# Layer B of a two-layer trunk: three direct pairs instead of four, and their low halves by accumulating DMAs instead of VectorE

## The chip, the cores and the metric

The kernel runs on one core of a Trainium2 chip. The metric is device time in microseconds of one execution. TensorE (PE in the profile) multiplies, VectorE (DVE) and ScalarE (ACT) work on what lies in SBUF and PSUM, GpSimd (POOL) does next to nothing here, SyncE (SP) issues the DMAs.

## The reference, cut to what matters

A sequence of 256 tokens, width 2048, passes two residual layers in float32, each with its norm, and a final norm:

```
p  = rms_norm(x, a_norm_g) @ a_w_in          # layer A: 2048 x 12288 -> u | v | z
x += (gelu(u) * mix(layer_norm(gelu(v))) * silu(z)) @ a_w_out
p  = rms_norm(x, b_norm_g) @ b_w_in          # layer B: 2048 x 20480 -> q,k,v three times | z
x += (attention(q, k, v; three dilations) * silu(z)) @ b_w_out
out = rms_norm(x, final_norm_g)
```

The change sits in the largest product, that with `b_w_in`: 256 x 2048 times 2048 x 20480.

## The kernel before

**Two halves of a number.** The kernel multiplies in the format fp32r. Each operand is split into a high half (the value cast to fp32r) and a low half (the value minus its high half), and `triple` (L229) makes one product of three matmuls: high times high, low times high, high times low. For weights the split is `split` (L126): ScalarE casts the raw tile to `wh`, and VectorE subtracts, `wl = raw - wh`.

**Slabs.** `slab` (L235) makes two 512-wide column blocks of the output, L and R, for both 128-token blocks. It walks over the 2048 rows of the weight in eight pairs of 128-row blocks. `load_pair` (L215) fetches a pair by two 512 KB DMAs on SP's queue into a `raw` tile of 128 x 2048 elements.

**Two kinds of pair.** A pair of kind "D" (direct) takes eight products, so 24 matmuls of 512 columns, and its weights need one cast and one subtraction of 2048 elements per partition. A pair of kind "S" takes seven products, so 21 matmuls, by a scheme in the manner of Strassen and Winograd. It needs sums of weight blocks first: VectorE makes `tsum` in three additions (L287 to L289), then 1536 elements of `raw` and 2048 of `tsum` are split, each by a cast and a subtraction. `KINDS_B` says which pairs are which and `ORDER_B` the order in which a slab walks over them. In layer B before, four of the eight are S, in the order D S D S S D S D. Layer B has 20 slabs (four quads of heads, five slabs each: three for q and k, two for v and z).

**Accumulators.** A slab holds seven accumulators, out of eight buffers in PSUM. When the last S pair has had its products, `early` (L261) combines three of them; the rest of the combinations (L309 to L317) follow at the slab's end, and `done` takes each result out on ScalarE.

**What sets the order.** The kernel is written in the Tile layer, whose scheduler fixes each engine's order at build time; an engine works its list in that order and waits on semaphores. Two pools bound how far work runs ahead of TensorE, and both hand out their buffers in turn, each new tile waiting for the one four allocations back:

```
wraw = ctx.enter_context(tc.tile_pool(name="wraw", bufs=NRAW))     # NRAW = 4: raw and tsum
wsp = ctx.enter_context(tc.tile_pool(name="wsp", bufs=NW))         # NW = 4: pairs wh, wl
```

A D pair takes one `raw` and one pair of `wh`, `wl`; an S pair takes two of each (`raw` and `tsum`; `wh`, `wl` and `vh`, `vl`). Small work between the slabs (transposes of q and k, scores, softmax, the product with v) is put between pairs by `later` and `tick`.

Of the kernel before, what the change touches and what calls it, by code (L numbers as in the profile page):

```python
# [9 lines left out]
F32 = mybir.dt.float32  # L10
F32R = mybir.dt.float32r
AF = mybir.ActivationFunctionType
ALU = mybir.AluOpType
AX = mybir.AxisListType

P = 128
D = 2048
S = 256
NT = S // P
EPS = 1e-6  # L20
AW = 4096
# [8 lines left out]
CW = 512  # L30
# [8 lines left out]
WARM2 = 11  # L39
NST = 11  # L40
NW = 4
NRAW = 4


KINDS_A, ORDER_A = "DDDSDSDS", (0, 1, 2, 3, 4, 5, 7, 6)
KINDS_B, ORDER_B = "DSDSDSDS", (0, 1, 2, 3, 5, 4, 7, 6)

# [21 lines left out]
def trunk(ctx, tc, x, a_norm_g, a_w_in, a_ln_g, a_ln_b, a_w_s, a_b_s, a_w_out,  # L69
          b_norm_g, b_w_in, b_w_out, final_norm_g, consts, out):  # L70
    nc = tc.nc
# [6 lines left out]
    opp = ctx.enter_context(tc.tile_pool(name="opp", bufs=8))  # L78
# [7 lines left out]
    def st(shape, name, dtype=F32):  # L86
        return stp.tile(shape, dtype, name=name, tag="st")
# [4 lines left out]
    ident = const.tile([P, P], F32, name="ident")  # L92
    tril = const.tile([P, P], F32, name="tril")
    dm0 = const.tile([P, NT, S], F32, name="dm0")
    dm12 = const.tile([P, 2, P], F32, name="dm12")
    rows = const.tile([P, P], F32, name="rows")
    cols = const.tile([P, P], F32, name="cols")
# [33 lines left out]
    class Operand:  # L131
# [9 lines left out]
        def alloc(self, kg):  # L141
            for part, d in (("h", self.hi), ("l", self.lo)):
                d[kg] = opp.tile([P, 13, P], F32R, name=f"{self.name}{part}{kg}", tag="op")
            self.at = {k: v for k, v in self.at.items() if k[0] // (KG // 2) != kg}
# [31 lines left out]
        def sums(self, kg, f, n):  # L176
            kinds = self.kinds[kg * (KG // 2) : (kg + 1) * (KG // 2)]
            sf = st([P, 6, P], f"{self.name}s")
            m = 0
            tt = nc.vector.tensor_tensor  # L180
            for i in range(KG // 2):
                q = f[:, 4 * i : 4 * i + 4, :]
                if kinds[i] == "D":
                    h = q.rearrange("p (k t) m -> p k t m", t=NT)
                    tt(out=sf[:, m : m + 2, :], in0=h[:, :, 0, :], in1=h[:, :, 1, :], op=ALU.subtract)
                    for j in range(2):
                        self.place(kg, i, ("d", j), n + m + j)
                    m += 2
                else:
                    a11, a21, a12, a22 = (q[:, b, :] for b in range(4))  # L190
                    for o, i0, i1 in ((0, a21, a22), (1, a11, sf[:, m]), (2, a21, a11), (3, a12, sf[:, m + 1])):
                        tt(out=sf[:, m + o, :], in0=i0, in1=i1, op=ALU.subtract)
                        self.place(kg, i, f"s{o + 1}", n + m + o)
                    m += 4
            split(sf[:, 0:m, :], self.hi[kg][:, n : n + m, :], self.lo[kg][:, n : n + m, :])
# [38 lines left out]

    def slab(h, w, cl, cr, dst, done, pre=None, fine=0):  # L235

# [32 lines left out]
        for n, i in enumerate(h.order):  # L269
            raw = load_pair(w, i, cl, cr, 1 if n < fine else 2)  # L270
            wh, wl = new_split()
            if h.kinds[i] != "S":
                if n >= fine:
                    split(raw, wh, wl)
# [80 lines left out]
    nc.vector.memset(ones, 1.0)  # L355
    nc.vector.memset(rows, 0.0)
    warm = small.tile([P, 1], F32, name="warm")
# [15 lines left out]
    with ExitStack() as actx:  # L373
        apool = actx.enter_context(tc.tile_pool(name="apool", bufs=1))

        xt = [st([P, NT, CW], f"x{kg}") for kg in range(4)]
# [53 lines left out]
        for c in range(0, NCH_A, 2):  # L430
# [8 lines left out]
            if c == 0:  # L439
                def pre(n):  # L440
# [13 lines left out]
                    nc.sync.dma_start(out=tril, in_=consts[:, P : 2 * P])  # L454
                    nc.sync.dma_start(out=dm0, in_=consts[:, 2 * P : 2 * P + NT * S].rearrange("p (b s) -> p b s", b=NT))
                    nc.sync.dma_start(out=dm12, in_=consts[:, 2 * P + NT * S :].rearrange("p (g s) -> p g s", g=2))
                    ssq = const.tile([P, NT, 4], F32, name="ssqa")
# [4 lines left out]
            else:  # L462
                pre = None
            slab(hA, a_w_in[0], AW + c * CW, AW + (c + 1) * CW, v2, v_done, pre, 2 if c == 0 else 0)
        mv = const.tile([P, NT, 2], F32, name="mv")
# [8 lines left out]
        for c in range(NCH_A):  # L474
# [3 lines left out]
            nc.sync.dma_start(out=wt, in_=a_w_s[0, c * G2 : (c + 1) * G2].rearrange("g t s -> t g s"))  # L478
            bs = apool.tile([P, G2, P], F32, name="bs", tag="bs", bufs=2)
            nc.sync.dma_start(out=bs, in_=a_b_s[0:1, c * G2 : (c + 1) * G2, :].broadcast_to([P, G2, P]))  # L480
# [45 lines left out]

            slab(hA, a_w_in[0], c * CW, 2 * AW + c * CW, uz, uz_done)
            g = st([P, KG, S], f"g{c}")
# [15 lines left out]


    gA = Operand("N" * (AW // P // 2), tuple(range(AW // P // 2)), "g")
    hB = Operand(KINDS_B, ORDER_B, "b")
# [110 lines left out]
    for q in range(NQUAD):  # L658
# [3 lines left out]
        for g in range(NG):  # L662
# [4 lines left out]

            slab(hB, b_w_in[0], 3 * g * D + q * CW, (3 * g + 1) * D + q * CW, qk, qk_done)
            qT, kT = st([P, KG, S], "qT"), st([P, KG, S], "kT")
# [13 lines left out]

        slab(hB, b_w_in[0], 2 * D + q * CW, 5 * D + q * CW, vs[:2], v_done)
        z = st([P, NT, CW], "zB")
# [6 lines left out]

        slab(hB, b_w_in[0], 8 * D + q * CW, 9 * D + q * CW, [vs[2], z], vz_done)

# [120 lines left out]
```

## Time and profile before

| | us |
|---|---|
| median of 3 runs (1747.61 to 1752.64) | 1751.72 |
| the profiled execution, its own time | 1750.36 |
| its span, first to last instruction | 1748.6 |
| TensorE busy in it | 1728.4 (99%) |
| VectorE busy in it | 1460.0 (83%) |
| ScalarE busy in it | 1025.9 (59%) |
| layer B's slabs, about 690 to 1625 us of the span: VectorE busy in these 935 us | 821.65 |

The profiled execution lies 1.4 us below the median, inside the spread of the runs, and 1.76 us of its time lie outside its span. The profile's busy share of TensorE counts overlapping matmuls, so it says that TensorE seldom stands still, not how fast it goes; its pace is read from the starts of successive matmuls. Names such as `bh` and `bl` are the high and low halves of layer B's input, `ah`, `gh`, `oh` those of other products.

### The profile page before, as it was taken

Reading aid. Unit: us, or ns where it says so; the run is one execution under the profiler, and the core shown is the slowest. Engines: PE = TensorE matmul, PEld = TensorE weight load, DVE = VectorE, ACT = ScalarE, POOL = GpSimd, SP = SyncE. Lnnn points to the kernel's source line nnn. Section 1 sums busy time; section 2 is a strip of 40 time slices with the busy share of each in tenths; the row PEclk is TensorE's granted clock in tenths of the full one; section 3 lists DMA queues with packets and bytes.
Section 4 is the critical chain, followed back from the end, with each engine's and each line's share of the span. In section 5 each row is a group of like instructions: output and inputs, shape, how many; then the busy total and the mean of one; then the engine's idle time right before and its main releaser. Section 6 shows DMA issues by size and latency. Waiting matters only on the chain.

```text
span 1748.6 us, 21067 instructions
## 1 busy us (share of the span) xinstructions
PE 1728.4 (99%) x8130; PEld 1434.7 (82%) x8130; DVE 1460.0 (83%) x1366; ACT 1025.9 (59%) x929; POOL 6.0 (0%) x9
## 2 busy tenths in 40 slices
PE   9999999999999999999999999999999999999998
PEld 7788888888888888788878888888888888888787
DVE  7988888999888555788989888988989988889753
ACT  7655765556566454555666555665556666556642
POOL 0000000000000000000000000000000000000000
PEclk9999999999999999999999999999999999999999
DMA  7666565555558575355656555555555456555871
GB/s 244 215 211 210 191 207 193 189 187 186 189 184 280 193 240 183 131 191 171 195 190 193 186 187 192 178 173 193 191 192 190 155 185 194 180 193 171 292 245 51
DMA packets 176404, 337.50 MB, mean 193 GB/s; under 512 B 10576, under 2 KB 14640, under 8 KB 176304
## 3 DMA queue, kind: packets, MB, share of 16 engines
q1 hardware_dynamic: 176304, 336.16, 58.1%
q8 instruction: 63, 1.03, 0.2%
q14 instruction: 37, 0.30, 0.1%
HBM read 330.35 MB, written 5.77 MB: 192 GB/s over the span
## 4 chain that ended last, share of the span: by engine, by line
PE 88%; DVE 5%; issue 2%; DMA 2%; ACT 2%; SPq 0%; ACTq 0%; DVEq 0%; POOLq 0%; POOL 0%
PE acc L231 27%; PE acc L233 27%; PE acc L232 27%; DVE wl L128 3%; DMA raw<-in_b_w_in_dram 1%; ACT wh L127 1%; PE pm L506 1%; PE sc L631 1%; PE pp L644 1%; PE po L703 1%; PE po L701 1%; PE sc L625 1%; PE tq L615 1%; DVE tsum L287 1%; PE tk L615 1%
## 5 line engine op out<-in xcount | busy, mean ns | idle before, releaser
L128 DVE TENSOR_TENSOR wl<-raw,wh 128x2048 fp32r<-128x2048 f32 (+2 forms) x306 | 633.0, 2069 | 114.9 <-ACT wh L127 112.1
L127 ACT CAST wh<-raw 128x2048 fp32r<-128x2048 f32 (+2 forms) x306 | 531.2, 1737 | 323.8 <-PE acc L232 252.5
L231 PE MATMUL acc<-wh,bh 128*128 128x512 f32 x1200 | 483.1, 403 | 3.6 <-ACT full L202 2.2
L233 PE MATMUL acc<-wl,bh 128*128 128x512 f32 x1200 | 470.2, 392 | 0.0
L232 PE MATMUL acc<-wh,bl 128*128 128x512 f32 x1200 | 468.6, 390 | 0.0
L127 ACT CAST wh<-tsum 128x2048 fp32r<-128x2048 f32 x116 | 221.7, 1911 | 209.3 <-DVE tsum L289 109.6
L128 DVE TENSOR_TENSOR wl<-tsum,wh 128x2048 fp32r<-128x2048 f32 x116 | 265.4, 2288 | 83.8 <-ACT wh L127 83.0
L231 PE MATMUL acc<-wh,ah 128*128 128x512 f32 x732 | 291.2, 399 | 2.8 <-ACT wh L127 2.8
L232 PE MATMUL acc<-wh,al 128*128 128x512 f32 x732 | 285.9, 391 | 0.7 <-DVE al L211 0.7
L233 PE MATMUL acc<-wl,ah 128*128 128x512 f32 x732 | 284.1, 391 | 2.0 <-DVE wl L128 2.0
L233 PEld LDWEIGHTS acc<-wl,bh 128*128 128x128 f32 x1200 | 225.6, 188 | 49.1 <-DVE wl L128 0.6
L231 PEld LDWEIGHTS acc<-wh,bh 128*128 128x128 f32 x1200 | 226.0, 188 | 47.3 <-ACT full L202 2.4
L232 PEld LDWEIGHTS acc<-wh,bl 128*128 128x128 f32 x1200 | 226.3, 189 | 43.7
L287 DVE TENSOR_TENSOR tsum<-raw 128x1024 f32<-128x1024 f32 x116 | 141.4, 1219 | 46.5 <-DMA raw<-in_b_w_in_dram 41.4
L231 PEld LDWEIGHTS acc<-wh,ah 128*128 128x128 f32 x732 | 138.2, 189 | 32.2 <-ACT wh L127 4.7
L233 PEld LDWEIGHTS acc<-wl,ah 128*128 128x128 f32 x732 | 137.4, 188 | 31.7 <-DVE wl L128 3.2
L232 PEld LDWEIGHTS acc<-wh,al 128*128 128x128 f32 x732 | 137.7, 188 | 28.9 <-DVE al L211 1.1
L231 PE MATMUL acc<-wh,gh 128*128 128x512 f32 x256 | 100.6, 393 | 0.0
L233 PE MATMUL acc<-wl,gh 128*128 128x512 f32 x256 | 99.8, 390 | 0.0
L232 PE MATMUL acc<-wh,gl 128*128 128x512 f32 x256 | 99.7, 389 | 0.0
L289 DVE TENSOR_TENSOR tsum<-tsum,raw 128x512 f32<-128x512 f32 x116 | 79.4, 685 | 1.0
L288 DVE TENSOR_TENSOR tsum<-tsum,raw 128x512 f32<-128x512 f32 x116 | 79.3, 683 | 0.8
(185 smaller groups left out, 1379.4 us busy)
## 6 DMA issues: line engine op xcount, KB each, us to landing
raw<-in_b_w_in_dram SPq DMA_DIRECT2D x320, 512.0 KB, 4.7
raw<-in_a_w_in_dram SPq DMA_DIRECT2D x188, 512.0 KB, 4.7
raw<-in_a_w_out_dram SPq DMA_DIRECT2D x64, 512.0 KB, 5.0
raw<-in_b_w_out_dram SPq DMA_DIRECT2D x16, 512.0 KB, 7.6
raw<-in_b_w_out_dram SPq DMA_DIRECT2D x8, 1024.0 KB, 5.1
raw<-in_a_w_in_dram SPq DMA_DIRECT2D x8, 256.0 KB, 6.1
rx<-in_x_dram SPq DMA_DIRECT2D x4, 512.0 KB, 7.6
x<-rx SPq DMA_DIRECT2D x4, 512.0 KB, 6.4
```

Of the source, the lines that this page charges most:

```text
L127: nc.scalar.copy(out=hi, in_=src)
L128: nc.vector.tensor_tensor(out=lo, in0=src, in1=hi.bitcast(F32), op=ALU.subtract)
L231: nc.tensor.matmul(acc, a[0], wh, start=start, stop=False)
L232: nc.tensor.matmul(acc, a[1], wh, start=False, stop=False)
L233: nc.tensor.matmul(acc, a[0], wl, start=False, stop=stop)
L287: tt(out=tsum[:, 0:2, :], in0=raw[:, 0:1, :].broadcast_to([P, 2, CW]), in1=raw[:, 1:3, :], op=ALU.add)
L288: tt(out=tsum[:, 2, :], in0=tsum[:, 0, :], in1=raw[:, 2, :], op=ALU.add)
L289: tt(out=tsum[:, 3, :], in0=tsum[:, 2, :], in1=raw[:, 3, :], op=ALU.add)
L506: nc.tensor.matmul(pm[:, f, t, :], v[:, t, fs], wsT[:, i, :], start=True, stop=True)
L615: nc.tensor.transpose(pt[:, f, t * P : (t + 1) * P], src[:, t, fs], ident)
L625: nc.tensor.matmul(sc[:, b, :], q[:, i, b * P : (b + 1) * P], k[:, i, :], start=True, stop=True)
L631: nc.tensor.matmul(sc[:, b, :], q[:, i, bs], k[:, i, bs], start=True, stop=True)
```

## The change

In layer B five of the eight pairs become S pairs and three stay D, in the order D S D S D S S S. For the D pairs, VectorE no longer makes the low half. ScalarE writes the high half twice, once as `wh` and once negated into `wl`, and then GpSimd issues two DMAs of 512 KB that add `raw` onto `wl` inside SBUF, one for each half of the tile. Layer A keeps its split (`DMA_A` is empty).

A group of two S pairs has 14 blocks where the largest group before had 13 (`NBLK`). To make room, `tril` and `rows` move into layer A's pool, `bs` goes from two buffers to one, and `dm0` and `dm12` are loaded after layer A into a pool of their own.

```
-KINDS_B, ORDER_B = "DSDSDSDS", (0, 1, 2, 3, 5, 4, 7, 6)
+DMA_A = ()
+DMA_B = (0, 2, 4)
+KINDS_B, ORDER_B = "SSDSDSDS", (2, 0, 4, 1, 6, 3, 5, 7)
...
             if h.kinds[i] != "S":
-                if n >= fine:
+                if n >= fine and n in dma:
+                    nc.scalar.copy(out=wh, in_=raw)
+                    nc.scalar.activation(out=wl, in_=raw, func=AF.Copy, scale=-1.0)
+                    for j in range(2):
+                        js = slice(2 * j, 2 * j + 2)
+                        nc.gpsimd.dma_start(out=wl[:, js, :], in_=raw[:, js, :], accum_op=ALU.add)
+                elif n >= fine:
                     split(raw, wh, wl)
...
-            bs = apool.tile([P, G2, P], F32, name="bs", tag="bs", bufs=2)
+            bs = apool.tile([P, G2, P], F32, name="bs", tag="bs")
...
+    bpool = ctx.enter_context(tc.tile_pool(name="bpool", bufs=1))
+    dm0 = bpool.tile([P, NT, S], F32, name="dm0")
+    dm12 = bpool.tile([P, 2, P], F32, name="dm12")
+    nc.sync.dma_start(out=dm0, in_=consts[:, 2 * P : 2 * P + NT * S].rearrange("p (b s) -> p b s", b=NT))
+    nc.sync.dma_start(out=dm12, in_=consts[:, 2 * P + NT * S :].rearrange("p (g s) -> p g s", g=2))
...
-            slab(hB, b_w_in[0], 3 * g * D + q * CW, (3 * g + 1) * D + q * CW, qk, qk_done)
+            slab(hB, b_w_in[0], 3 * g * D + q * CW, (3 * g + 1) * D + q * CW, qk, qk_done, dma=DMA_B)
```

`n` counts a pair's place in the slab, so the three D pairs stand at places 0, 2 and 4, and each has its low half made by DMA.

The first place is ScalarE where the first slab of layer B ends and the second begins. The numbers behind the names tell tiles apart; `raw_6030` before and `raw_6060` after are the weights of the new slab's first pair. Before:

```order
L127 CAST wh_5954<-tsum_5948 128x2048 [waits DVE_49,PE_49,Activation_49]
L127 CAST wh_5989<-raw_5986 128x2048 [waits DMAHW0_49,DMAHW7_49,PE_49,Activation_49]
L127 CAST wh_6033<-raw_6030 128x2048 [waits DMAHW1_49,DMAHW2_49,PE_49,Activation_49]
L127 CAST wh_6068<-raw_6065 128x1536 [waits DMAHW3_49,DMAHW4_49,PE_49,Activation_49]
L262 COPY k_5698<-acc_5749 128x512
```

After:

```order
L126 CAST wh_6011<-raw_6008 128x1536 [waits DMAHW0_49,DMAHW7_49,PE_49,Activation_49]
L126 CAST wh_6019<-tsum_6013 128x2048 [waits DVE_49,PE_49,Activation_49]
L273 CAST wh_6063<-raw_6060 128x2048 [waits DMAHW1_49,DMAHW2_49,PE_49,Activation_49]
L274 ACTIVATE wl_6064<-raw_6060 128x2048 [waits DMASW5_49,DMASW4_49,PE_49]
L261 COPY k_5717<-acc_5770 128x512 [waits PE_49]
```

The pair ahead of the slab's end is now an S pair, the D pair has a second pass over 2048 elements on ScalarE, and the copy of `early` comes behind both.

The second place is GpSimd's queue, which issues the DMAs of three D pairs one after the other; the last two rows are those of the pair above.

```order
L277 DMA wl_5810<-raw_5806 128x1024 [waits DMASW1_49,DMAHW5_49,DMASW0_49,DMAHW6_49,DVE_49,Activation_49]
L277 DMA wl_5810<-raw_5806 128x1024
L277 DMA wl_5891<-raw_5887 128x1024 [waits DMASW3_49,DMAHW1_49,DMASW2_49,DMAHW2_49,DVE_49,Activation_49]
L277 DMA wl_5891<-raw_5887 128x1024
L277 DMA wl_6064<-raw_6060 128x1024 [waits DMASW5_49,DMAHW1_49,DMASW4_49,DMAHW2_49,DVE_49,Activation_49]
L277 DMA wl_6064<-raw_6060 128x1024
```

Before, this queue held none of these rows; each first DMA waits for ScalarE's negated high half, and each second is issued right behind it.

The third place is TensorE at the start of the same slab. Before:

```order
L233 MATMUL acc_5718<-wl_5990,bh3_5372 128x512
L231 MATMUL acc_6037<-wh_6033,bh0_4826 128x512 [waits Activation_49]
L232 MATMUL acc_6037<-wh_6033,bl0_4827 128x512
L233 MATMUL acc_6037<-wl_6034,bh0_4826 128x512 [waits DVE_49]
L231 MATMUL acc_6041<-wh_6033,bh0_4826 128x512 [waits DVE_49]
```

After:

```order
L232 MATMUL acc_5731<-wl_6020,bh3_5380 128x512
L230 MATMUL acc_6069<-wh_6063,bh1_4930 128x512 [waits DVE_49,Activation_49]
L231 MATMUL acc_6069<-wh_6063,bl1_4931 128x512
L232 MATMUL acc_6069<-wl_6064,bh1_4930 128x512 [waits DMASW4_49,Activation_49]
L230 MATMUL acc_6073<-wh_6063,bh1_4930 128x512 [waits Activation_49]
```

The third matmul of the slab waited for VectorE's subtraction; it now waits for the first of the two accumulating DMAs (`DMASW4`).

## Rows read from the trace of the kernel before

**Rows 1.** The page: span; busy time by engine; the chain of waits by engine.

```profile
span 1748.6 us, 21067 instructions
...
PE 1728.4 (99%) x8130; PEld 1434.7 (82%) x8130; DVE 1460.0 (83%) x1366; ACT 1025.9 (59%) x929; POOL 6.0 (0%) x9
...
PE 88%; DVE 5%; issue 2%; DMA 2%; ACT 2%; SPq 0%; ACTq 0%; DVEq 0%; POOLq 0%; POOL 0%
```

**Rows 2.** Busy us by stretch of layer B, granted clock, DMA share, GB/s.

```profile
core 0: us, PE busy (x) PEld busy (x) DVE busy (x) ACT busy (x) POOL busy (x), PEclk, DMA share, GB/s
...
1100.00:1300.00 200.00, 200.00 (x965) 166.43 (x964) 176.40 (x162) 123.00 (x112) 0.00 (x0) 1.00 0.55 182
...
sum 935.00, PE 931.13 PEld 773.04 DVE 821.65 ACT 564.29 POOL 0.80; mean PE 186.23 PEld 154.61 DVE 164.33 ACT 112.86 POOL 0.16
```

**Rows 3.** Timeline of TensorE over one D pair of layer B, 24 matmuls.

```profile
1105.55 0.39 PE L231 MATMUL acc<-wh,bh 128*128 128x512 f32 x1
1105.77 0.39 PE L232 MATMUL acc<-wh,bl 128*128 128x512 f32 x1
...
1110.79 0.39 PE L233 MATMUL acc<-wl,bh 128*128 128x512 f32 x1
```

**Rows 4.** Groups by line and form: busy, mean ns | idle before, releaser.

```profile
L128 DVE TENSOR_TENSOR wl<-raw,wh 128x2048 fp32r<-128x2048 f32 x186 | 425.2, 2286 | 97.5 <-ACT wh L127 96.6
L127 ACT CAST wh<-raw 128x2048 fp32r<-128x2048 f32 x186 | 355.2, 1910 | 199.7 <-PE acc L232 159.1 <-issue 23.2 <-DMA raw<-in_b_w_out_dram 7.6
...
L128 DVE TENSOR_TENSOR wl<-tsum,wh 128x2048 fp32r<-128x2048 f32 x116 | 265.4, 2288 | 83.8 <-ACT wh L127 83.0
...
L127 ACT CAST wh<-tsum 128x2048 fp32r<-128x2048 f32 x116 | 221.7, 1911 | 209.3 <-DVE tsum L289 109.6 <-PE acc L232 95.2 <-PE pp L644 2.7
L128 DVE TENSOR_TENSOR wl<-raw,wh 128x1536 fp32r<-128x1536 f32 x116 | 203.1, 1751 | 10.6 <-ACT wh L127 8.9 <-PE acc L233 1.5
L127 ACT CAST wh<-raw 128x1536 fp32r<-128x1536 f32 x116 | 172.0, 1483 | 122.9 <-PE acc L232 93.4 <-issue 18.7 <-ACT kT L616 6.2
L287 DVE TENSOR_TENSOR tsum<-raw 128x1024 f32<-128x1024 f32 x116 | 141.4, 1219 | 46.5 <-DMA raw<-in_b_w_in_dram 41.4 <-DMA raw<-in_a_w_in_dram 4.9
...
L289 DVE TENSOR_TENSOR tsum<-tsum,raw 128x512 f32<-128x512 f32 x116 | 79.4, 685 | 1.0
...
L666 ACT ACTIVATE q<-q,rQ 128x512 f32<-128x512 f32 x24 | 17.2, 717 | 25.1 <-DVE q L309 25.1
```

**Rows 5.** Waits from 700 to 1620 us: total us, times, longest.

```profile
ACT wh L127 <- PE acc L232: 149.3, 72, 4.0
...
DVE tsum L287 <- DMA raw<-in_b_w_in_dram: 41.4, 19, 4.2
```

**Rows 6.** DMA issues: KB each, median us to landing; last row all `raw`.

```profile
raw<-in_b_w_in_dram SPq DMA_DIRECT2D x320, 512.0 KB, 4.7
...
raw<-in_b_w_out_dram SPq DMA_DIRECT2D x8, 1024.0 KB, 5.1
...
out_dram<-x SPq DMA_DIRECT2D x6, 256.0 KB, 2.3
...
ident<-in_consts_dram SPq DMA_DIRECT2D x1, 64.0 KB, 2.0
...
DMA to landing us min/median/max: 3.5/4.7/11.0
```

**Rows 7.** Waits of SP's queue behind the bias of layer A.

```profile
SPq L222 <- DVE bias L510: 48.5, 16, 4.9
...
SPq L480 <- DVE bias L510: 10.4, 5, 2.1
```

More of the change, by code (lines that the diff above doesn't have):

```diff
@@ L40 @@
 NST = 11
+NBLK = 14
 NW = 4
@@ L92, in trunk @@
     ident = const.tile([P, P], F32, name="ident")
[L93 to L96, printed above, removed]
     cols = const.tile([P, P], F32, name="cols")
@@ L142, in alloc @@
             for part, d in (("h", self.hi), ("l", self.lo)):
-                d[kg] = opp.tile([P, 13, P], F32R, name=f"{self.name}{part}{kg}", tag="op")
+                d[kg] = opp.tile([P, NBLK, P], F32R, name=f"{self.name}{part}{kg}", tag="op")
             self.at = {k: v for k, v in self.at.items() if k[0] // (KG // 2) != kg}
@@ L177, in sums @@
             kinds = self.kinds[kg * (KG // 2) : (kg + 1) * (KG // 2)]
-            sf = st([P, 6, P], f"{self.name}s")
+            sf = st([P, 8, P], f"{self.name}s")
             m = 0
@@ L233, in triple, with slab @@
         nc.tensor.matmul(acc, a[0], wl, start=False, stop=stop)
-    def slab(h, w, cl, cr, dst, done, pre=None, fine=0):
+    def slab(h, w, cl, cr, dst, done, pre=None, fine=0, dma=()):
         acc, left = {}, {}
@@ L355, in trunk @@
     nc.vector.memset(ones, 1.0)
-    nc.vector.memset(rows, 0.0)
     warm = small.tile([P, 1], F32, name="warm")
@@ L374, in trunk @@
         apool = actx.enter_context(tc.tile_pool(name="apool", bufs=1))
+        tril = apool.tile([P, P], F32, name="tril")
+        rows = apool.tile([P, P], F32, name="rows")
+        nc.vector.memset(rows, 0.0)
         xt = [st([P, NT, CW], f"x{kg}") for kg in range(4)]
@@ L454, in pre @@
                     nc.sync.dma_start(out=tril, in_=consts[:, P : 2 * P])
-                    nc.sync.dma_start(out=dm0, in_=consts[:, 2 * P : 2 * P + NT * S].rearrange("p (b s) -> p b s", b=NT))
-                    nc.sync.dma_start(out=dm12, in_=consts[:, 2 * P + NT * S :].rearrange("p (g s) -> p g s", g=2))
                     ssq = const.tile([P, NT, 4], F32, name="ssqa")
@@ L463, in trunk @@
                 pre = None
-            slab(hA, a_w_in[0], AW + c * CW, AW + (c + 1) * CW, v2, v_done, pre, 2 if c == 0 else 0)
+            slab(hA, a_w_in[0], AW + c * CW, AW + (c + 1) * CW, v2, v_done, pre, 2 if c == 0 else 0, () if c == 0 else DMA_A)
         mv = const.tile([P, NT, 2], F32, name="mv")
@@ L525, in uz_done @@
                                      scale=rA[:, t : t + 1])
-            slab(hA, a_w_in[0], c * CW, 2 * AW + c * CW, uz, uz_done)
+            slab(hA, a_w_in[0], c * CW, 2 * AW + c * CW, uz, uz_done, dma=DMA_A)
             g = st([P, KG, S], f"g{c}")
@@ L682, in v_done @@
             nc.scalar.activation(out=vs[side][:, t, :], in_=ap, func=AF.Copy, scale=rB[:, t : t + 1])
-        slab(hB, b_w_in[0], 2 * D + q * CW, 5 * D + q * CW, vs[:2], v_done)
+        slab(hB, b_w_in[0], 2 * D + q * CW, 5 * D + q * CW, vs[:2], v_done, dma=DMA_B)
         z = st([P, NT, CW], "zB")
@@ L691, in vz_done @@
                 nc.scalar.activation(out=z[:, t, :], in_=ap, func=AF.Silu, scale=rB[:, t : t + 1])
-        slab(hB, b_w_in[0], 8 * D + q * CW, 9 * D + q * CW, [vs[2], z], vz_done)
+        slab(hB, b_w_in[0], 8 * D + q * CW, 9 * D + q * CW, [vs[2], z], vz_done, dma=DMA_B)
         def values(b, vs=vs, z=z, pTs=pTs, dens=dens):
```

## The prediction

> **What bounds the kernel now.** First the page: TensorE is busy in 99% of the span and makes 88% of the chain of waits, VectorE 5% [rows 1]. So TensorE's own work sets the time, and what others do costs only where TensorE waits for it. Second the stretches of layer B: in the 935 us of its 20 slabs TensorE is idle for 4 us, VectorE is busy for 822 us (88%), ScalarE for 564 (60%), and the DMA engines for 0.55 of a typical stretch, at 182 GB/s; the granted clock is 1.00, the level of 2.4 GHz [rows 2]. Third the timeline of one D pair, for the pace: 24 matmuls start between 1105.55 and 1110.79, so one every 5.24 / 23 = 0.228 us, whatever the 0.39 us that the profile gives each [rows 3]. A D pair is 24 x 0.228 = 5.47 us of TensorE, an S pair 21 x 0.228 = 4.78. A slab is 180 x 0.228 = 41.0 us; with 935 / 20 = 46.75 us per slab, 5.7 are left for transposes, scores and the like, 0.7 per pair. Fourth the waits of layer B: ScalarE stands 149 us in 72 waits until TensorE has read a `wl`-and-`wh` buffer to its end [rows 5]. The splits thus run as far ahead as four buffers let them and no further, and that lead is what a slower low half has to fit into.
>
> **What the change takes away.** Per slab 180 matmuls become 3 x 24 + 5 x 21 = 177, in 20 slabs 60 fewer: 60 x 0.228 = **-13.7 us**, all on the path. VectorE loses 80 subtractions of 2.29 us (183) and gains 20 S pairs of 1.22 + 2 x 0.685 + 1.75 + 2.29 = 6.63 us (133) [rows 4]: 50 us less in layer B, 772 of some 921, so it stays under TensorE. Its gain is worth nothing by itself, since TensorE did not wait for it.
>
> **What it adds on ScalarE.** 20 S pairs instead of D add 1.48 + 1.91 - 1.91 us each, 30 in all, and each of 60 D pairs a second pass over 2048 elements. No row shows an ACTIVATE of that size. A cast of it takes 1.91 us, and four ACTIVATEs of 512 elements 4 x 0.717 = 2.87 [rows 4]; these are the ends, and I take 1.91, since size and memory are the same. That makes 115 us, ScalarE 709 of 921 us (77%): hidden as busy time, but it delays the DMAs behind it.
>
> **What it adds on the path: a wait for a DMA.** Of each product the third matmul reads `wl`, so TensorE now waits for an accumulating DMA where it waited for a subtraction. Behind it in TensorE's list stand all later products; behind a late TensorE the next buffers, so ScalarE's casts, VectorE's sums, and on SP the loads into the `raw` tile that the DMA still reads. GpSimd's queue holds only these DMAs in the slabs.
>
> How long may it take? At place 0 the buffer is the one that the S pair at place 6 of the slab before used first; TensorE has read it after 9 of that pair's 21 matmuls. To its own third matmul the new pair then has 12 + 21 + 2 matmuls, 7.97 us, and some 1.0 of small work, 9.0. ScalarE takes 2 x 1.91 of it and mostly one evacuation of 0.72 ahead of them. **4.4 us** stay for the first DMA, and, since the second half is read 12 matmuls later, 4.4 + 2.7 = 7.1 for both. At places 2 and 4 the buffer comes free at the end of an S pair, and a D and an S pair lie between: 47 matmuls, 10.7 us, with small work 12.1, less 3.8 and 0.7 to 1.4: about **7** for the first and 9.7 for both.
>
> How long will it take? GpSimd issues no DMA in this trace, and nothing accumulates. The nearest rows are SP's plain ones: 64 KB land in 2.0 us, 256 KB in 2.3, 512 KB in 3.5 at the fastest and 4.7 in the middle, 1024 KB in 5.1 [rows 6]. That is near 1.8 us plus 3.3 per 1024 KB, and 1.2 more for 512 KB beside the weights' traffic. An accumulating DMA must read its destination too, so the DMA engines read 1024 KB for 512 KB. The lower end is that this costs nothing: 3.5 us, and 3.5 + 1.65 for both. The upper end is the slowest load of all, 11.0 [rows 6], and 11.0 + 3.3 for both. I take the row with the same bytes read, 5.1, plus 1.2 for the traffic: 6.3 for the first. The second reads 3.3 us longer: 9.6, or 10.8 if the traffic costs it as much again; I take 10.2.
>
> No row shows what an add costs a DMA. The Trainium skill, "Collectives: The Full Stack", section "The bandwidth ceiling: the fold count and why AG ≠ RS ≠ AR", says that the reduce runs at half the rate of the copy (31 against 62 GB/s), not for the adding but because it reads two sources over the same read ring. By it each transfer's data time doubles, and the sum below stays as it is; were the second read free, the lower end would hold and the time be 1737.
>
> The stall, then: at place 0 the larger of 6.3 - 4.4 and 10.2 - 7.1, 3.1 us; at places 2 and 4 the larger of 0 and 10.2 - 9.7, 0.5 each. 4.1 us per slab, in 20 slabs **+82**.
>
> **What else moves, at nothing.** `bs` with one buffer: SP's DMA for a chunk waits for the bias of the chunk just before instead of two before, and stands one weight load earlier in the list. That wait was 10.4 us in five times, at most 2.1 [rows 7], and the loads queued behind it are covered, since in all of layer A VectorE waited 4.9 us for weights [rows 4]; without cover it costs 7 x 2.1 = 15. `dm0` and `dm12` are two small loads amid those of `a_w_out`, long before use. `early` now follows the last pair, so that three accumulators come free some 2 us later; the D pair that starts the next slab needs four buffers and finds the combinations under way. One wait of 1 us per slab would be 20, and goes into the range.
>
> **Sum**, against the profiled execution's 1750.4 (1.4 below the median of the runs): 1750.4 - 13.7 + 82 = **1819 us**. With both DMAs at the lower end nothing waits: 1737. At the upper end place 0 stalls for 14.3 - 7.1 = 7.2 and the others for 4.6 each, 16.4 x 20 = 328: 2065.
>
> **Rivals.**
> Hidden: the DMAs land within 4.4 and 7.1 us, and the time is 1736.7 to some 1742, faster. This is decided at place 0, by the first DMA's 4.4 us. For it speaks that the fastest 512 KB load took 3.5 us and that SBUF to SBUF may be quicker than from memory off the chip; against it, that two are in flight together, each with two reads, where 512 KB of plain load take 4.7 in the middle. The Trainium skill, "DMA: Bandwidth & Descriptors", section "Anatomy of one DMA — SWDGE (gpsimd) path", has 2.0 us plus bytes at 436 GB/s for a DMA from GpSimd, 3.2 us for 512 KB, 4.4 for 1024 KB; by that rule the first DMA is just hidden and this rival holds. No run here shows it.
>
> Draw: stalls of about 0.7 us per slab eat the gain, 1743 to 1769.
>
> The DMA engines become the bound: at 3.3 us of data per accumulating DMA 120 of them add 396 us to 0.55 x 935 = 514, 910 of some 921 us. If an add costs three passes rather than two, 120 x 4.95 = 594, layer B takes at least 1108 us in place of 935 - 14, and the time is 1737 + 187 = 1924 or more. For it speaks how near 910 is to 921; against it, that no row tells how much of the 0.55 is data and how much a packet's wait.
>
> **How the numbers follow.** Forecast, 1770 to 1880: 0.45. Hidden: 0.22. Draw: 0.07. DMA bound, or a latency toward the upper end, 1880 to 2065: 0.26, a little over half of it below 1950. The range from 1736 to 1950 leaves out some 0.13. A measurement of this kernel can tell 0.3%, about 5 us, from no change. Faster by more: hidden and a quarter of the draw, 0.24; the same 0.03; slower 0.73. The forecast's own range is 1770 to 1880.
>
> **What would show it.** Right: in the profile after, 60 matmuls fewer at an unchanged 0.228 us; TensorE's waits at L232 put down to `wl` by DMA, largest at the first pair of a slab; accumulating DMAs that land in 6 us or more; VectorE's busy share in layer B lower, ScalarE's near 77%; layer A unchanged to within 5 us. Wrong: DMAs that land in 4 us, and TensorE without waits for them; or idle time of TensorE behind weight loads, with a DMA share near 1, which is the third rival; or waits at the slab's first matmul, for `early`.

## The result, and the profile after

The changed kernel takes 1909.59 us in the median of four runs (1902.78 to 1915.38); the kernel before, run beside it, 1752.18 (1747.61 to 1752.91). The ratio is 1.0906, with a 95% interval of 1.0873 to 1.0938: slower by 157 us, where 1819 had been forecast, slower by 68. The direction was right. The forecast's own range, 1770 to 1880, did not hold the time (the wide one of 1736 to 1950 did), and the rise that was forecast is less than half of the measured one.

The page after, as in [rows 1]:

```profile
span 1905.3 us, 21569 instructions
...
PE 1774.2 (93%) x8070; PEld 1444.2 (76%) x8070; DVE 1423.4 (75%) x1390; ACT 1160.0 (61%) x1010; POOL 109.9 (6%) x129
...
PE 55%; DMA 23%; DVE 8%; ACT 6%; issue 6%; SPq 1%; POOL 0%; ACTq 0%; DVEq 0%; POOLq 0%
```

The 60 matmuls are gone (8130 to 8070), and TensorE's share of the chain falls from 88% to 55%: the DMAs now hold 23% of it, where they held 2%. Layer A is unchanged: layer B's first product starts at 727.1 us, before at 727.8. The typical stretch of layer B, against [rows 2]:

```profile
1100.00:1300.00 200.00, 179.79 (x827) 144.77 (x826) 143.32 (x144) 127.51 (x110) 18.00 (x21) 0.96 0.77 212
```

827 matmuls in 200 us in place of 965, a granted clock of 0.96 in place of 1.00, a DMA share of 0.77 in place of 0.55. VectorE, thought to lose only a little work, falls from 176 us to 143: it starves too. The waits from 700 to 1780 us, against [rows 5] (first TensorE, VectorE and ScalarE, then SP's queue):

```profile
DVE tsum L292 <- DMA raw<-in_b_w_in_dram: 198.2, 65, 6.1
ACT wh L126 <- PE acc L231: 117.0, 47, 6.3
PE acc L232 <- DMA wl<-raw: 63.9, 44, 4.6
...
SPq L221 <- DMA wl<-raw: 471.7, 42, 12.7
SPq L221 <- DVE wl L127: 269.0, 70, 10.1
```

The forecast wait is there, third in the list. Above it stands VectorE, which waits 198 us for weights where it waited 41. The last two rows are waits of SP's queue, which issues all loads in order, for a free `raw` tile; 472 us of them end only when an accumulating DMA has landed. The queue waited about as long before, but for VectorE (here 700 to 1620 us):

```profile
SPq L222 <- DVE wl L128: 639.4, 127, 12.9
```

So the total is no loss by itself. What is new is what frees the tile; that this makes the weights late is seen at VectorE, and in the chain below. DMA queues and landing times, against [rows 6] (packets, MB, share of the engines' span; then KB each, us to landing):

```profile
q1 hardware_dynamic: 176304, 336.16, 53.5%
q0 software_dynamic: 17280, 62.92, 17.1%
...
raw<-in_b_w_in_dram SPq DMA_DIRECT2D x320, 512.0 KB, 4.9
...
wl<-raw POOLq DMA_DIRECT2D x120, 512.0 KB, 8.6
```

Worked out from the 60 pairs of accumulating DMAs in the trace: from the issue of a pair's first DMA the first lands after 7.5 us in the median (4.6 to 9.8), both have landed after 10.0 (7.7 to 12.7). Weight loads land hardly later than before (4.9 against 4.7); they are issued later.

The chain of waits over two such DMAs (start us, duration us, what) shows all three costs in 40 us:

```profile
1305.42 4.94 DMA wl<-raw
1310.37 0.14 issue
1310.50 0.77 PE acc L232
1311.27 0.43 PE acc L230
...
1315.96 0.43 PE acc L232
1316.39 0.27 PE acc L230
1316.65 0.23 PE acc L231
...
1327.24 1.82 ACT wl L274
1329.06 0.28 issue
1329.34 0.43 POOL wl L277
1329.77 0.11 issue
1329.88 9.09 DMA wl<-raw
1339.09 0.37 SPq L221
1339.51 4.80 DMA raw<-in_b_w_in_dram
1344.40 1.24 DVE tsum L292
```

At 1310.50 TensorE's third matmul starts when the DMA lands, the forecast stall. Then twelve matmuls go at 0.43 us each and only after 1316.39 at 0.23. And from 1329.88 the next accumulating DMA holds its `raw` tile for 9.09 us; only then is the next load issued into that tile, 4.80 us more, and only then VectorE begins the sums of the next S pair. The granted clock of these matmuls (columns as in [rows 2]):

```profile
1305.42:1309.50 4.08, 2.07 (x10) 1.38 (x8) 4.05 (x5) 4.08 (x4) 1.75 (x2) 1.00 0.93 219
1309.50:1316.30 6.80, 5.80 (x14) 4.57 (x15) 5.36 (x7) 4.26 (x4) 1.75 (x2) 0.50 1.03 265
1316.30:1319.86 3.56, 3.56 (x18) 2.90 (x17) 1.23 (x1) 1.51 (x2) 0.00 (x0) 0.99 0.98 255
```

Ahead of and through the stall TensorE was idle for some 3 us; the granted clock is then 0.50, the level of 1.2 GHz, for the matmuls behind it too, and 0.99 again after them. In the whole trace it stands at 0.50 for 106 us in 22 places; before, for 12 us in 3.

TensorE's lost time from 690 us on, worked out from the starts of successive matmuls in each trace (what goes beyond the usual distance, by what the matmul waited for; pace is the loss of matmuls that waited for nothing, over 0.15 us each; small is the rest):

| us | third matmul of a product | other waits | pace | small | time |
|---|---|---|---|---|---|
| before | 0.0 | 6.8 | 4.6 | 10.0 | 1752.2 |
| no accumulating DMA (e8_noadd, below) | 0.0 | 10.5 | 6.4 | 11.0 | 1742.7 |
| the change | 74.9 | 54.9 | 43.1 | 19.6 | 1909.6 |

So of the 164.5 us by which the change's span exceeds that without the DMAs, 75 are the forecast stall, 44 other waits, 45 the slow pace and the small rest (36.7 + 8.6). This tells where the time went, not what it would give back to take one of them away.

### The profile page after: what moved, and what is told of

It reads as the page before. It is cut to its first block, busy times and chain, and to the rows that moved or that the text cites. A ratio compares the mean times of both kernels' runs of the same rounds, so it can differ in the third digit from the quotient of the medians.

```text
span 1905.3 us, 21569 instructions
## 1 busy us (share of the span) xinstructions
PE 1774.2 (93%) x8070; PEld 1444.2 (76%) x8070; DVE 1423.4 (75%) x1390; ACT 1160.0 (61%) x1010; POOL 109.9 (6%) x129
## 4 chain that ended last, share of the span: by engine, by line
PE 55%; DMA 23%; DVE 8%; ACT 6%; issue 6%; SPq 1%; POOL 0%; ACTq 0%; DVEq 0%; POOLq 0%
PE acc L232 17%; PE acc L231 17%; PE acc L230 17%; DMA wl<-raw 12%; DMA raw<-in_b_w_in_dram 11%; DVE wl L127 4%; ACT wl L274 2%; ACT wh L273 1%; DVE tsum L292 1%; ACT wh L126 1%; SPq L221 1%; DVE tsum L293 1%; PE pm L511 1%; ACT Sh L661 1%; PE po L713 1%
## 5 line engine op out<-in xcount | busy, mean ns | idle before, releaser
L126 ACT CAST wh<-raw 128x1536 fp32r<-128x1536 f32 (+2 forms) x246 | 408.1, 1659 | 325.6 <-PE acc L231 214.2
L127 DVE TENSOR_TENSOR wl<-raw,wh 128x1536 fp32r<-128x1536 f32 (+2 forms) x246 | 485.7, 1975 | 131.3 <-ACT wh L126 126.8
L232 PE MATMUL acc<-wl,bh 128*128 128x512 f32 x1180 | 482.0, 409 | 66.7 <-DMA wl<-raw 63.9
L230 PE MATMUL acc<-wh,bh 128*128 128x512 f32 x1180 | 491.6, 417 | 5.5 <-ACT vB L261 3.3
L126 ACT CAST wh<-tsum 128x2048 fp32r<-128x2048 f32 x136 | 259.6, 1909 | 224.0 <-PE acc L231 107.2
L127 DVE TENSOR_TENSOR wl<-tsum,wh 128x2048 fp32r<-128x2048 f32 x136 | 311.1, 2288 | 79.1 <-ACT wh L126 78.6
L292 DVE TENSOR_TENSOR tsum<-raw 128x1024 f32<-128x1024 f32 x136 | 166.4, 1224 | 225.1 <-DMA raw<-in_b_w_in_dram 198.2
L277 POOL DMA_DIRECT2D wl<-raw x120 | 105.1, 1035 | 1447.0 <-ACT wl L274 1117.6
L273 ACT CAST wh<-raw 128x2048 fp32r<-128x2048 f32 x60 | 114.4, 1907 | 34.5 <-PE acc L231 25.5
L274 ACT ACTIVATE wl<-raw 128x2048 fp32r<-128x2048 f32 x60 | 114.6, 1910 | 0.0
```

The source lines that it names most:

```text
L126: nc.scalar.copy(out=hi, in_=src)
L127: nc.vector.tensor_tensor(out=lo, in0=src, in1=hi.bitcast(F32), op=ALU.subtract)
L230: nc.tensor.matmul(acc, a[0], wh, start=start, stop=False)
L232: nc.tensor.matmul(acc, a[0], wl, start=False, stop=stop)
L273: nc.scalar.copy(out=wh, in_=raw)
L274: nc.scalar.activation(out=wl, in_=raw, func=AF.Copy, scale=-1.0)
```

## The experiments

The theory after this reading: lateness costs, and by three ways at once, the third matmul, the held `raw` tile, and the clock. Rivals: the DMAs' bytes; TensorE's direct wait alone; the fifth S pair and its order. Each kernel is the changed one with the edit shown, seen once (the change's own four runs lie within 12.6 us, so smaller differences from it are not read); the kernel before took 1752.17 beside e1 to e4, 1747.12 beside e5 to e8, 1752.81 beside e9 to e12, 1749.67 beside e13 to e16, 1747.91 beside e17 and e18.

**What stays when the DMAs go.**

```
-                    for j in range(2):
-                        js = slice(2 * j, 2 * j + 2)
-                        nc.gpsimd.dma_start(out=wl[:, js, :], in_=raw[:, js, :], accum_op=ALU.add)
```

> Leaves out the accumulating DMAs altogether: the low half stays the negated high half. What is left of the change is the fifth S pair, the order, ScalarE's second pass and the small moves. The prediction's price of those is 1736.7 on 1750.4, so 1737. Theory from the tiny DMAs (1759.9): the pattern itself costs, 1745 to 1760. Rival (the tiny DMAs' latency of 3.7 us is what costs there): 1735 to 1742.

1742.69, just above the rival's bounds. The same stretch as above:

```profile
1100.00:1300.00 200.00, 199.96 (x964) 166.36 (x963) 171.80 (x171) 150.02 (x128) 0.00 (x0) 1.00 0.55 187
```

TensorE is full again, at a clock of 1.00. The five S pairs, the order, ScalarE's second pass, `bs` and `early` together cost 6 us over the 1736.7 of the sum: pricing them at nothing was right, and all else is the accumulating DMAs. This trace also shows the room that the prediction worked out, from the end of ScalarE's second pass to TensorE's first reading of each half: in the median 4.2 and 6.9 us at place 0, 7.0 and 9.7 at place 2, 7.2 and 10.2 at place 4.

**Short DMAs, and late ones without bytes.** Two DMAs of 64 KB (e1), and five of 64 KB one after the other (e5):

```
-nc.gpsimd.dma_start(out=wl[:, js, :], in_=raw[:, js, :], accum_op=ALU.add)
+nc.gpsimd.dma_start(out=wl[:, 2 * j, :P], in_=raw[:, 2 * j, :P], accum_op=ALU.add)    # e1; e5: for j in (0, 1, 0, 1, 1)
```

> The accumulating DMAs move 128 of 1024 columns each (64 KB instead of 512 KB), so most of the low half stays the negated high half; waits, order and instructions stay as in the change. Theory, that the loss comes from the DMAs being late at TensorE and from what follows from that: a 64 KB transfer lands within the 4.4 us that place 0 leaves, TensorE's waits at L232 fall from 74 us to under 10, the clock stays at 1.00, and the time is 1737 to 1755. Rival, that the new order (three S pairs and the early combination at the slab's end, a second pass on ScalarE) costs time by itself: 1780 or more with the DMAs nearly free.

1759.92. Both DMAs land 4.2 us after the first issue. It ends 5 us above what was expected, 17 above no DMA.

> Leaves out: of each low half of a DMA'd D pair only a few columns are completed. Instead of two accumulating DMAs of 512 KB each such pair gets five of 64 KB on the same two column blocks, one after the other (0, 1, 0, 1, 1), so that the last lands about as late as the full ones (three chained at 3.7 us, some 11 us), while next to no bytes move; raw is held and TensorE waits as in the change. Theory (lateness: the raw tile is held and TensorE's third matmul waits): 1820 to 1860. Rival (the bytes, which slow the weight loads and everything else): 1760 to 1790, near the 1759.9 of one tiny DMA for each half.

1918.8, well above what the theory itself expected. The last of the five lands 11.3 us after the first issue, and the whole loss is there, with a third of the bytes:

```profile
q0 software_dynamic: 43200, 19.68, 9.0%
...
wl<-raw POOLq DMA_DIRECT2D x300, 64.0 KB, 3.0
```

Lateness is enough. The same chain without TensorE's wait (the three matmuls read `wh` in place of `wl`):

> As e5_chain, but the three matmuls that would read the low half of a DMA'd D pair read the high half, so TensorE waits for no accumulating DMA; raw is still held by the chain. Theory (the hold of raw binds, as the removal of TensorE's wait alone gave nothing with full DMAs): within 15 us of e5_chain. Rival (TensorE's own wait is what the lateness costs): 50 us or more below e5_chain, 1760 to 1790.

1871.1, between the two expectations: TensorE's wait is worth 48 here, and 128 remain over no DMA.

**Bytes alone.** The DMAs add one spare tile onto another:

```
+src = bpool.tile([P, 512], F32, name="src")          # spare[0]
+sink = bpool.tile([P, 2, 512], F32, name="sink")     # spare[1]
...
+nc.gpsimd.tensor_copy(out=spare[0][:, 0:1], in_=wl[:, 0, 0:1].bitcast(F32))
...
-nc.gpsimd.dma_start(out=wl[:, js, :], in_=raw[:, js, :], accum_op=ALU.add)
+nc.gpsimd.dma_start(out=spare[1], in_=spare[0].unsqueeze(1).broadcast_to([P, 2, 512]), accum_op=ALU.add)
```

> Leaves the low halves incomplete: the two accumulating DMAs of 512 KB of each D pair run as often as in the change, started by a GpSimd copy of one column of wl, but they add one spare tile onto another, so that no tile of the kernel is held by them and nobody waits for them. Against the 1742.7 with no accumulating DMA at all. Theory A (the bytes cost by themselves: e3_traffic's 1841 against 1760 with tiny ones): 1800 to 1840. Theory B (only lateness costs, what is held or waited for until the landing): 1740 to 1760.

1779.07, between the two again: 36 us over no DMA. The stretch:

```profile
1100.00:1300.00 200.00, 193.20 (x913) 158.91 (x912) 164.75 (x166) 146.93 (x128) 35.04 (x37) 0.98 0.93 245
```

The DMA share is 0.93, above the change's 0.77, and TensorE still makes 913 matmuls there against 827. The DMA engines are not the bound of the change. (These DMAs all write one tile, so that they follow one another; two in flight at once were not tried without holds. One hold is left: GpSimd's copy of a column reads `wl` and waits for the DMAs of the pair before, and VectorE waits 10 us for it. So the 36 us need not be the bytes' alone.)

**TensorE's wait, taken away or put off.** In e2 the third matmuls read `wh` in place of `wl`; in e11 they stand behind the sixteen others of their pair:

```
-product(key, h.block(i, a), wh[:, o, :], wl[:, o, :])
+product(key, h.block(i, a), wh[:, o, :], (wh if n >= fine and n in dma else wl)[:, o, :])     # e2
+product(key, h.block(i, a), wh[:, o, :], wl[:, o, :], held)                                   # e11
+if j and held:
+    thirds(held)                  # for key, a, wl, stop in held: nc.tensor.matmul(acc[key], a[0], wl, ...)
```

> TensorE reads the high half in place of the low half in the D pairs whose low half comes by DMA, so it no longer waits for these DMAs; they still run at full size and still hold the raw buffers. Theory, that of some 170 us of stalls 74 are the direct wait, 50 the lower clock after it and 50 the work that the held raw buffers make late: 1770 to 1800, clock 0.99 to 1.00, VectorE still waiting over 120 us for weights. Rival A, that all of it is the direct wait: 1737 to 1750. Rival B, that the held buffers and the traffic are the main loss: 1840 or more.

> Nothing left out. In the DMA'd D pairs TensorE does the sixteen matmuls that read wh first and the eight that read wl last, so the first low half is needed 14 x 0.228 = 3.2 us later, the second 1.4 us later; DMAs and holds are unchanged. Theory (raw's hold binds, as e2_nowait at 1911.8 said): within 15 us of 1909. Rival (TensorE's wait for the DMA, 74 us at L232, is what costs): 1840 to 1870.

1911.84 and 1910.83: nothing gained either time, as the second rival of e2 and the theory of e11 had it. The waits of e2:

```profile
DVE tsum L292 <- DMA raw<-in_b_w_in_dram: 210.5, 58, 8.1
PE acc L232 <- DVE wl L127: 49.0, 22, 5.7
...
SPq L221 <- DMA wl<-raw: 354.6, 32, 14.2
```

TensorE waits at the same line, now for VectorE's low halves of the S pairs, whose weights came late. Its wait for the DMA had covered the wait for VectorE.

**The hold of `raw`, taken away,** by a DMA that reads `wh`; TensorE waits for it (e7) or not (e3):

```
-nc.gpsimd.dma_start(out=wl[:, js, :], in_=raw[:, js, :], accum_op=ALU.add)
+nc.gpsimd.dma_start(out=wl[:, js, :], in_=wh[:, js, :].bitcast(F32), accum_op=ALU.add)
```

> Changes the result's low halves: the two full accumulating DMAs read wh in place of raw, so raw is free after ScalarE's second pass, while TensorE waits for the DMAs as in the change. Theory (hold of raw costs some 70, the direct wait is one wait that takes the place of another): 1841 to 1870, near e3_traffic's 1841. Rival (the direct wait adds its own 74 us to the traffic's 1841): about 1915.

1900.35: 9 us less, no more than the change's runs differ, and nearer to the rival's 1915 than to the theory; its third matmuls cost TensorE 114 us in place of 75.

> As the run without TensorE's wait, and the DMAs take the high half instead of raw as their source, so raw is free once ScalarE has read it: the same bytes move, and nothing waits for them but the buffer's next use. Theory: traffic alone costs little, 1737 to 1760, VectorE's wait for weights under 80 us. Rival, that 63 MB of extra traffic slows the weight loads: 1780 or more, with weight loads landing in over 5.5 us in the middle.

1841.41: with hold and wait both gone 68 us are gained, where e2 and e7 gained 0 and 9. Either of the two by itself costs nearly what both cost together; and 99 us over no DMA remain without either. It was read at first as 80 us of traffic over e1; e9 with its 36 does not bear that out. What e3 still holds are `wh` and `wl` themselves (ScalarE and VectorE wait 70 us for these DMAs in it). How the 99 us divide between those holds and the bytes was not measured.

**What makes them late: the add.** The DMAs copy:

```
-nc.gpsimd.dma_start(out=wl[:, js, :], in_=raw[:, js, :], accum_op=ALU.add)
+nc.gpsimd.dma_start(out=wl[:, js, :], in_=raw[:, js, :])
```

> Changes the low halves: the two DMAs copy raw into wl instead of adding it; bytes, tiles held and waits are those of the change. If the add costs a DMA its second read, as the prediction had it, the copy lands in 3.5 to 5 us and 5 to 7 for both, and the time is 1760 to 1800. Rival (adding costs nothing beside copying): landing times as in the change, 7.5 and 10.0, and within 15 us of 1909.

1794.64. The copies land after 5.6 us, both after 6.9:

```profile
q0 software_dynamic: 17280, 62.92, 9.6%
...
wl<-raw POOLq DMA_DIRECT2D x120, 512.0 KB, 5.9
```

The same packets and bytes take 0.096 x 1792.8 / 120 = 1.43 us of the DMA engines for a copy and 0.171 x 1905.3 / 120 = 2.71 for an add, 1.9 times as long. The Trainium skill, "Collectives: The Full Stack", section "The bandwidth ceiling: the fold count and why AG ≠ RS ≠ AR", has a reduce at half the rate of a copy, for its second read; by that rule the ratio is 2, and these traces agree with the ratio; the reason for it they don't show. Holds and waits being the same, 3.1 us less of lateness (10.0 to 6.9) go with 115 us less of time: 0.62 us for each of 60 pairs and each us, with what the shorter use of the DMA engines is worth in it.

**Fewer or other late halves.** Only the second half of each D pair by DMA (e13), GpSimd in place of ScalarE's second pass and the DMAs (e14), place 0 by VectorE (e16):

```
+split(raw[:, js, :], wh[:, js, :], wl[:, js, :])     # e13: j = 0; j = 1, made ahead of it, keeps ScalarE's pass and its DMA
+nc.gpsimd.tensor_tensor(out=wl[:, js, :], in0=raw[:, js, :], in1=wh[:, js, :].bitcast(F32), op=ALU.subtract)   # e14
-DMA_B = (0, 2, 4)
+DMA_B = (2, 4)     # e16
```

> Nothing left out. Of each of the three D pairs only the second half tile has its low half by an accumulating DMA, one of 512 KB alone in flight; VectorE subtracts the first half, which is needed first. The second half is read 12 matmuls after the first, where the prediction gave 7.1 us of room at place 0. Lateness theory: one DMA lands in some 5 us (4.6 was the fastest of the change's), so nothing or little waits: 1745 to 1775. Rival (the bytes cost 36 us for 120 DMAs, and any wait of a DMA the same again): 1790 to 1830.

1858.17. One DMA alone in flight lands after 7.5 us, not 5; both expectations fell. TensorE's third matmuls stand idle 9.6 us for these DMAs and 24.2 for VectorE's low halves.

> Nothing left out. At place 0 VectorE subtracts as before; places 2 and 4 keep the DMAs. Prediction's working: place 0 carries 3.1 of the 4.1 us of stall a slab, so three quarters of the loss goes: 1760 to 1800. Rival (the hold of the raw tile matters at every place, and VectorE gets 46 us more work): 1850 to 1900.

1895.54, the rival's value. TensorE's third matmuls, from 700 to 1780 us:

```profile
PE acc L232 <- DMA wl<-raw: 57.3, 30, 4.0
...
PE acc L232 <- DVE wl L127: 18.7, 27, 1.6
```

The two places left wait 57 us for their DMAs, where all three waited 64 and these two had 22 of the 75 in the table; to this comes VectorE, which is late too.

> Nothing left out. GpSimd subtracts in place of ScalarE's second pass and the DMAs: wl = raw - wh, 1024 columns at a time. No DMA, no bytes; the lateness is GpSimd's time, which no run so far shows. If two such subtractions take under 7 us together: 1740 to 1760, and not slower than before; if 10 us or more: 1880 to 1930, as the change, since the same tiles are held and waited for.

1895.9. Two operations take 6.2 us (first row), so that 1740 to 1760 had been expected; this fell. Where GpSimd works, VectorE's own additions become slower. The same line (mean ns behind the comma) in e14:

```profile
L276 POOL TENSOR_TENSOR wl<-raw,wh 128x1024 fp32r<-128x1024 f32 x120 | 367.7, 3087 | 1190.4 <-ACT wh L273 1082.9 <-DVE wl L127 74.1 <-PE acc L231 20.1
...
L292 DVE TENSOR_TENSOR tsum<-tsum,raw 128x512 f32<-128x512 f32 x136 | 160.4, 1179 | 2.5
```

and in the change, where it has the number 293:

```profile
L293 DVE TENSOR_TENSOR tsum<-tsum,raw 128x512 f32<-128x512 f32 x136 | 93.5, 687 | 2.4
```

In e14's trace the 33 of these 136 additions that overlap a GpSimd subtraction take 2.72 us in the mean, the 103 others 0.69.

**DMAs earlier.** ScalarE writes `wl` before `wh`, alone (e10) and with the third matmuls last (e12):

> Nothing left out. ScalarE writes the negated half before wh, so that both DMAs start 1.9 us earlier, their bytes unchanged. Theory (lateness costs, at TensorE's third matmul and at the raw tile): the 74 us of waits at L232 fall by up to 1.9 us a slab at place 0 and at place 4, and the clock's loss with them: 1820 to 1870. Rival (bytes, or a ring that takes the time up again): within 15 us of 1909.

> Nothing left out. The negated half first and the third matmuls last: the DMAs start 1.9 us earlier and the low halves are needed 3.2 and 1.4 us later. If lateness at TensorE is the cost, the stalls of 2.6 us a slab at place 0 and 0.7 at place 4 are gone and so is the clock's loss: 1780 to 1830. If the raw ring or the bytes are: near e10_negated_first, within 15 us.

1933.93 and 1957.87: slower by 24 and 48. Both expectations fell. In e10 a pair's DMAs land 9.1 us after the first issue at place 0 and 11.5 and 11.9 at places 2 and 4 (9.0, 11.3 and 10.0 in the change), and SP's queue waits 87 us for other loads of `raw`, where it waited 12. Why an earlier start ends later was not settled. (ScalarE then makes `wh`, for which the first matmuls wait, 1.9 us later.)

**The fifth S pair alone, and the DMAs alone.** In e4 VectorE makes all low halves (`DMA_B = ()`); in e17 the kinds and order are those of the kernel before, with DMAs at three of its four D pairs; in e18 the five S pairs stand as S D S S D S S D.

```
+KINDS_B, ORDER_B = "DSDSDSDS", (0, 1, 2, 3, 5, 4, 7, 6)      # e17, DMA_B = (0, 2, 5)
+KINDS_B, ORDER_B = "SSDSDSDS", (0, 2, 1, 3, 4, 5, 7, 6)      # e18, DMA_B = (1, 4, 7)
```

> The five S pairs in the same order, the low halves of the D pairs by VectorE as before, no DMA on GpSimd. Theory, that VectorE becomes the bound: its work in layer B grows from 822 to 822 + 20 x (6.63 - 2.29) = 909 us against 921 of TensorE, so 1745 to 1800. Rival, that it still hides: 1737 to 1742, and the change's DMAs were not needed.

1820.06, above both expectations. In the stretch of [rows 2] VectorE is busy for 181 us of 200, not all of it, but ScalarE waits 200 us for its sums where it waited 84, and TensorE for both (29 us for ScalarE's casts, 17 for VectorE's low halves). So with five S pairs VectorE's subtractions no longer hide, at 909 us of some 921 as worked out.

> Nothing left out. The kinds and order of the kernel before (four S pairs, D S D S S D S D) with the DMAs at the first three D pairs, places 0, 2 and 5; VectorE splits the last D pair as before. VectorE is freed of 60 subtractions of 2.29 us and gains nothing, so it has 137 us more room. Theory A (lateness costs because VectorE, with five S pairs, loses the lead that it needs): 1760 to 1790. Theory B (the ring of raw tiles and TensorE's wait cost by themselves, whatever VectorE has to do): 1840 to 1900.

1826.0, between the theories: the DMAs cost 78 us even where VectorE has 137 us more room than before. Its waits:

```profile
DVE tsum L292 <- DMA raw<-in_b_w_in_dram: 150.3, 52, 7.6
...
PE acc L232 <- DMA wl<-raw: 34.1, 37, 3.6
...
SPq L221 <- DMA wl<-raw: 285.5, 36, 14.7
```

> Nothing left out. The change with its five S pairs, the order S D S S D S S D in place of D S D S D S S S, all three D pairs by DMA. Theory A (in the change's order three S pairs stand last, 3 x 6.63 us of VectorE against 3 x 4.78 of TensorE, and the late ring takes the lead for them away): 1800 to 1850. Theory B (the ring and TensorE's wait cost by themselves, in any order): within 25 us of 1909.

1888.85: 21 us less than the change, in the bounds of the second theory. So the DMAs cost in either order. With four S pairs they cost 78 us, with five about twice as much; that VectorE's load makes this difference is likely, but e17 differs in the number of S pairs and in the order at once.

No version beat the kernel before by more than a measurement of it can tell; only e8, which leaves the low halves of three pairs undone, lies 4 us below it.

## Why the prediction was right or wrong

**The gain, and what was priced at nothing: right.** 1742.7 without the DMAs (e8), against 1736.7. ScalarE's second pass takes 1.91 us, the value taken, and its busy time rose by 134 us where 145 were worked out.

**The latency: near.** 6.3 and 10.2 us were taken, 7.5 and 10.0 measured in the median of all places. That an add costs the DMA engines twice a copy was right too (2.71 against 1.43 us; 3.3 and 1.65 had been taken).

**The stall at the third matmul: right in size, in part by luck.** 3.1 us at place 0 and 0.5 at places 2 and 4 make 62, 10 and 10 us; put to the last landing before the wait's end, the trace has 52, 6.7 and 14.9, 74 together against 82. But the sum took the second DMA of a pair as the one that is waited for at all three places, and about 67 of the 74 us end with the first.

**The step that failed** is the paragraph on the path: it names what stands behind a late `wl`, "ScalarE's casts, VectorE's sums, and on SP the loads into the `raw` tile that the DMA still reads", and prices only the stall. The sum had one term where the trace has three: 75 us at the third matmul, 44 of other waits, mostly of transposes and scores for VectorE and ScalarE that ran late, and 45 of pace, most of it matmuls at half the clock. The room itself (4.4 and 7.1 us, 7 and 9.7) was worked out rightly for a kernel in which nothing is late, as e8 shows. (The 935 us from 690 on were taken for the slabs; the products with `bh` run from 728 to 1642 us, 45.7 us a slab instead of 46.75, which moves the room by some 0.1.) But it is not a property of a place: where loads are late the splits don't run as far ahead, and a stall at one place changes what the next has. e16 moved the stall from place 0 to the others instead of ending it.

Rows of before could not have priced it fully. A D pair held its `raw` tile from the load's issue for 4.7 + 1.91 + 2.29 = 8.9 us at the least; now for 4.7 + 2 x 1.91 + 10.2 = 18.7. A slab takes 13 tiles of this ring of four, so at 46 us a slab a tile may be held for 4 x 46 / 13 = 14.2 us in the mean. 18.7 is above that, but the S pairs' tiles are held for less, and since the buffers are handed out in turn the mean counts; by shortest holds from the same rows (10.5 us for an S pair's `raw`, 6.8 for its `tsum`) it is 11.0, and the ring would still have sufficed. Measured, from the load's issue (for `tsum` from its first addition) to the end of the last reader, a D pair's tile was held for 12.8 us without the DMAs (e8) and 24.5 in the change; the 13 tiles of a slab were held for 164 us together in e8 and for 193 in the change, and four buffers have 4 x 46 = 184 in a slab of the old pace. So the change does not fit into the ring at that pace. The measured holds contain waits that the lateness itself made, so this is an account after the fact and not a price; that lateness costs without TensorE's wait for the DMA is shown by e2 and e6, at 1911.8 and 1871.1.

**The rivals.** Hidden was wrong by the latency: at place 0, where 4.4 us had been left for the first DMA, it landed 6.4 us after ScalarE's second pass in the median. The Trainium skill, "DMA: Bandwidth & Descriptors", section "Anatomy of one DMA — SWDGE (gpsimd) path", gave 3.2 us for 512 KB; the traces do not agree for adds, of which none of 512 KB landed under 4.5 us, and copies took 3.0 at the fastest and 5.6 in the median (the first of a pair). The DMA engines as the bound: wrong, since e9 reaches a share of 0.93 at 1779.07 us.

**What stays open.** The share of each way in the change's own time: taking away TensorE's wait gains nothing, freeing `raw` 9, both 68, so the terms hide one another; and of the 99 us that then remain it is open how much is the hold of `wh` and `wl`, whose ring has four buffers too. A fifth buffer for `raw`, which would have tested the ring directly, was not tried. Nor was the clock kept up through a stall to price it by itself.

## What to carry to other kernels

When an operation is replaced by a slower path, price every resource it holds until it ends: not only who reads the result, but the source tile in its ring, and what an in-order queue of loads does behind that ring. Compare the mean time that tiles are held with buffers x period / tiles per period. Read slack from a trace only as long as the lead that made it survives the change, and add the loss of pace after each stall.

## What was not expected of the hardware

- An accumulating DMA from SBUF to SBUF takes 1.9 times the engine time of a copy (2.71 against 1.43 us for 512 KB) and lands in 7.5 us at the median in the change, the first of two, and also in e13, alone. In the change it took 6.1 us where two weight loads overlapped it (6 of the 60) and 8.8 where four did (37). In e17 it took 4.6 in the median with as many loads beside it; what decides it is open. GpSimd takes 1.04 us in the mean to issue one, 0.53 for a copy.
- In the change the granted clock stands at 0.50 in 22 places, 106 us in all, as around the stall that ends at 1310.50, and stays there while TensorE works again at 0.43 us a matmul: pace and the small rest are about a quarter of the loss (45 of 164.5).
- A GpSimd subtraction of 1024 columns takes 3.09 us, and VectorE's 512-column additions in the same kernel took 1.18 in place of 0.69 us in the mean. The Trainium skill, "SBUF — State Buffer", section "SBUF: two separate sides", has GpSimd and a VectorE operation with two SBUF inputs take turns at a shared pair of ports, each for the whole instruction; e14 agrees, since only the additions that overlap a GpSimd subtraction are slow (2.72 us against 0.69).
